# A hybrid decoder layer on one core: the groups' stage written as a fixed order of slots on three engines

## The chip, the core and the metric

The kernel runs on one core of a Trainium2 chip. Four engines of that core matter here: TensorE (PE in the profile) multiplies matrices into PSUM, ScalarE (ACT) evaluates functions and copies, VectorE (DVE) does arithmetic on tiles, and SyncE (SP) issues the loads of the weights. GpSimd (POOL) issues a few other loads. Each engine has its own list of instructions and works through it in order; an instruction that needs another engine's result waits on a semaphore, and everything behind it on that engine waits too. The metric is the time of one execution of the program on the device, in microseconds (us).

## The reference: what is computed

The layer takes 512 tokens of width 1024 with 16 learned tokens in front (528 positions). After a norm, one projection gives five parts: a pooled branch, the gate `z`, the inputs `x`, `B`, `C` of a state-space branch (Mamba-2, in chunks of 128 tokens), the step `dt`, and two sets of sigmoid gates. The state-space branch has 32 heads of 64 channels in 8 groups of 4 heads:

```python
xbc = silu(causal_depthwise_conv(xbc, conv_w, conv_b))       # x, B, C; 4 taps
a_cs = cumsum(dt * a) per chunk
lmat = exp(a_cs[l] - a_cs[s]) for s <= l, else 0             # decay between two tokens
y_diag = (C B^T * lmat) @ (x * dt)                           # inside a chunk
states = B^T @ (exp(a_cs[-1] - a_cs) * x * dt)               # what a chunk hands on
y_off  = C @ state_before * exp(a_cs)
y = (y_diag + y_off + x * d_skip) * silu(z)
y = y * rsqrt(mean(y * y over the group's 256 channels) + eps) * norm_w
```

The result of the 8 groups goes through `w_ssd_out`, is merged with the pooled branch by the gates, goes through `w_o` onto the residual, and an MLP with squared ReLU and a last norm follow. All is float32; products are made of a high and a low part of each operand (three products instead of one), so every block of weights is split on the chip into `whi` (a cast on ScalarE) and `wlo` (a subtraction on VectorE).

## The kernel before

**Blocks of weights.** All weights come as blocks of 128 x 1024. `block()` hands out the next one; `depth[0]` says how many more are loaded and split ahead of it, which is 2 in the groups' stage. A block is a load (SP, into one of three `raw` buffers), the cast on line 75 and the subtraction on line 76; `whi` and `wlo` have four buffers each.

**The groups' stage.** It is a loop over the 8 groups, one round each. In a round, the scan of group g (`ssd`, lines 397 to 522) and the projections of group g+1 (`group_proj`, line 364) are woven together. The scan's parts are: transposes of x and B (lines 413 to 434, tiles `ptb`, `ptm`, `ptx`), the decays (`eb`, lines 445 to 456: the exponentials, and between them the differences of cumulated decays in place in `abc`), the products C B^T and the states (`pcb`, `pst`), the outputs (`po` from the states, `py` from the masked decays), their gathering into `yt` on VectorE (lines 495 to 499), the sum of squares by a product with ones (`png`), and the norm and the split of the result into `yh` and `yl`. The projections are four tiles `px` (B, C and two of x, 48 products each, of 264 or 258 columns), a tile `pz` of twice 24 products of 512 columns, and in some rounds a gate `pgp` of 24 such products. A `px` tile goes through `conv` (line 342): one activation on ScalarE, three multiply-adds on VectorE that read it from PSUM, and a SiLU on ScalarE.

**Rounds that differ.** Round 4 also multiplies the first 8 results with half of `w_ssd_out` (`out_half`, tiles `pso`, copied on ScalarE to `acc`), and round 7 has no projections and multiplies results 8 to 13 instead (`out_part`, tiles `psp`, added on VectorE to `acc`). `GATE_AT` says which rounds have a gate.

**What sets the order.** Both parts are generators, and `weave` runs them in turn by the counts of `STEPS`: that is the order on TensorE alone (`manual_schedule` names PE only). On ScalarE and VectorE the framework's scheduler picks the order by its own estimate of when operands are ready. PSUM holds two tiles of 1024 columns (`psum2`, for `px`, `pz`, `pgp`, `pso`, `psp`) and four of 512 (`psum1`, for the scan); a tile is written anew when what read the old one is done.

## Time and profile before

| | us |
|---|---|
| median of three runs | 1037.05 (1034.16 to 1037.66) |
| the profiled execution | 1034.4 |
| its span, first to last instruction | 1032.7 |
| groups' stage in it (first transposes of round 0 to the end of the last `psp` tile) | 66.9 to 485.4 |
| busy in the span: PE, DVE, ACT | 1007.3, 714.5, 562.7 |

A matrix product is shown as busy until its modelled end, which lies after the start of the next one, so a full row of PE says that products follow each other, not that they are at their peak. PEclk is the clock that was granted to TensorE; below 1.00 its products take longer. A row of the view of waits says who waited for whom, for how long in total, how often, and the longest wait.

### The profile page before, as it was taken

Reading aid. Unit: us, or ns where it says so; the run is one execution under the profiler, and the core shown is the slowest. Engines: PE = TensorE matmul, PEld = TensorE weight load, DVE = VectorE, ACT = ScalarE, POOL = GpSimd, SP = SyncE. Lnnn points to the kernel's source line nnn. Section 1 sums busy time; section 2 is a strip of 40 time slices with the busy share of each in tenths; the row PEclk is TensorE's granted clock in tenths of the full one; section 3 lists DMA queues with packets and bytes.
Section 4 is the critical chain, followed back from the end, with each engine's and each line's share of the span. In section 5 each row is a group of like instructions: output and inputs, shape, how many; then the busy total and the mean of one; then the engine's idle time right before and its main releaser. Section 6 shows DMA issues by size and latency. Waiting matters only on the chain.

```text
span 1032.7 us, 14079 instructions
## 1 busy us (share of the span) xinstructions
PE 1007.3 (98%) x5689; PEld 874.0 (85%) x5689; DVE 714.5 (69%) x950; ACT 562.7 (54%) x748; POOL 88.6 (9%) x52
## 2 busy tenths in 40 slices
PE   9999999999889999989999999999999999999997
PEld 8888889898678898968899888888888888888886
DVE  7988676776535585967756457875777567666866
ACT  7774959577526629582334333374554345454444
POOL 0100000000000000000000000002131422403400
PEclk9999999999899999999999999999999999999999
DMA  6243141423322231413532333324323323233112
GB/s 236 73 156 105 34 148 41 144 62 128 97 76 109 87 118 42 144 37 106 205 102 83 104 100 100 125 82 146 100 82 122 105 92 110 102 103 123 41 42 82
DMA packets 29281, 105.62 MB, mean 102 GB/s; under 512 B 3296, under 2 KB 4256, under 8 KB 28192
## 3 DMA queue, kind: packets, MB, share of 16 engines
q1 hardware_dynamic: 26496, 92.75, 27.7%
q0 software_dynamic: 2000, 11.08, 2.8%
q8 instruction: 44, 0.72, 0.3%
q10 hardware_dynamic: 720, 0.91, 0.3%
q14 instruction: 21, 0.17, 0.1%
HBM read 102.55 MB, written 2.16 MB: 101 GB/s over the span
## 4 chain that ended last, share of the span: by engine, by line
PE 82%; ACT 9%; DVE 6%; issue 2%; DMA 1%; SPq 0%; ACTq 0%; DVEq 0%
PE pf L96 6%; PE pf L98 6%; PE pf L97 6%; PE px L154 4%; PE px L155 4%; PE px L157 4%; PE alpha L985 3%; PE alpha L987 3%; PE alpha L986 3%; PE pz L154 2%; PE pz L157 2%; PE pz L155 2%; PE pp L157 1%; PE pp L154 1%; PE pp L155 1%
## 5 line engine op out<-in xcount | busy, mean ns | idle before, releaser
L76 DVE TENSOR_TENSOR wlo<-raw,whi 128x1024 fp32r<-128x1024 f32 (+1 forms) x131 | 163.3, 1252 | 146.8 <-ACT whi L75 146.8
L75 ACT CAST whi<-raw 128x1024 fp32r<-128x1024 f32 (+1 forms) x131 | 135.7, 1043 | 219.2 <-PE pf L97 55.8
L154 PE MATMUL px<-uh,whi 128*128 128x264 f32 (+1 forms) x448 | 120.2, 289 | 4.1 <-DVE bt L347 2.5
L155 PE MATMUL px<-ul,whi 128*128 128x264 f32 (+1 forms) x448 | 117.3, 283 | 0.0
L96 PE MATMUL pf<-vh,whi 128*128 128x512 f32 x256 | 99.8, 390 | 0.0
L98 PE MATMUL pf<-vh,wlo 128*128 128x512 f32 x256 | 99.6, 389 | 0.0
L97 PE MATMUL pf<-vl,whi 128*128 128x512 f32 x256 | 99.6, 389 | 0.0
L157 PE MATMUL px<-uh,wlo 128*128 128x264 f32 (+1 forms) x448 | 90.4, 283 | 0.0
L154 PEld LDWEIGHTS px<-uh,whi 128*128 128x128 f32 x448 | 84.7, 189 | 5.7 <-issue 3.7
L155 PEld LDWEIGHTS px<-ul,whi 128*128 128x128 f32 x448 | 84.4, 188 | 0.2
L747 DVE TENSOR_TENSOR slo<-b,shi 128x1024 fp32r<-128x1024 f32 x35 | 49.2, 1404 | 31.6 <-ACT shi L746 31.6
L157 PEld LDWEIGHTS px<-uh,wlo 128*128 128x128 f32 x448 | 68.8, 188 | 0.0
L746 ACT CAST shi<-b 128x1024 fp32r<-128x1024 f32 x35 | 36.8, 1050 | 47.3 <-PE pf L97 36.4
L98 PEld LDWEIGHTS pf<-vh,wlo 128*128 128x128 f32 x256 | 48.1, 188 | 10.0
L97 PEld LDWEIGHTS pf<-vl,whi 128*128 128x128 f32 x256 | 48.1, 188 | 10.0
L96 PEld LDWEIGHTS pf<-vh,whi 128*128 128x128 f32 x256 | 48.1, 188 | 9.8
L996 POOL TENSOR_TENSOR b<-b,b 128x1024 f32<-128x1024 f32 x14 | 35.5, 2539 | 238.3 <-DVE slo L747 238.3
L985 PE MATMUL alpha<-shi,hh 128*128 128x512 f32 x140 | 54.6, 390 | 0.0
L987 PE MATMUL alpha<-shi,hl 128*128 128x512 f32 x140 | 54.5, 389 | 0.0
L986 PE MATMUL alpha<-slo,hh 128*128 128x512 f32 x140 | 54.5, 389 | 0.0
L812 DVE TENSOR_TENSOR ht<-ht,alpha 128x1024 f32<-128x1024 f32 x35 | 42.6, 1217 | 10.9 <-PE alpha L987 10.9
L154 PE MATMUL pz<-uh,whi 128*128 128x512 f32 x112 | 44.0, 392 | 1.8 <-DVE xc L347 1.4
(419 smaller groups left out, 2497.8 us busy)
## 6 DMA issues: line engine op xcount, KB each, us to landing
raw<-in_w SPq DMA_DIRECT2D x129, 512.0 KB, 3.5
b<-in_w SPq DMA_DIRECT2D x28, 512.0 KB, 3.5
abc<-acs_d POOLq DMA_DIRECT2D x8, 1024.0 KB, 5.6
wob<-in_w SPq DMA_DIRECT2D x8, 512.0 KB, 5.2
xt<-in_xT SPq DMA_DIRECT2D x8, 264.0 KB, 5.9
ht<-in_x POOLq DMA_DIRECT2D x4, 512.0 KB, 6.2
w<-in_w SPq DMA_DIRECT2D x4, 512.0 KB, 3.5
out_dram<-out SPq DMA_DIRECT2D x4, 320.0 KB, 2.4
```

Source lines behind the costliest of these rows:

```text
L75: act.copy(hi[:, c], raw[:, c])
L76: dve.tensor_tensor(lo[:, c], raw[:, c], hi[:, c].bitcast(F32), op=ALU.subtract)
L96: pe.matmul(ps, ah, bh, start=first, stop=False)
L97: pe.matmul(ps, ah, bl, start=False, stop=False)
L98: pe.matmul(ps, al, bh, start=False, stop=last)
L154: pe.matmul(o, wh, rhs[0][k][:, c], start=k == 0, stop=False)
L155: pe.matmul(o, wh, rhs[1][k][:, c], start=False, stop=False)
L157: pe.matmul(o, wl, rhs[0][k][:, c], start=False, stop=k == NK - 1)
L747: dve.tensor_tensor(lo, src, hi.bitcast(F32), op=ALU.subtract)
L985: pe.matmul(ps[t], a[0], wh[:, cs], start=f, stop=False, skip_group_check=True)
L986: pe.matmul(ps[t], a[0], wl[:, cs], start=False, stop=False, skip_group_check=True)
L987: pe.matmul(ps[t], a[1], wh[:, cs], start=False, stop=l, skip_group_check=True)
```

## The change

The generators and `weave` go. The scan becomes a class `Scan` with a method for each part, and one loop calls these parts and the projections in a written order. `manual_schedule` now names PE, Activation and DVE, so that this order is kept on all three engines, the splits of the weights and the copies of `acc` included.

- The SiLU of B, C and x leaves `conv` and is done for the three tiles at the end of the round, x in one instruction (`silus`).
- All 16 decay differences of a round are Relu activations on ScalarE (`spans`); before, 8 were there and 8 on VectorE (line 453). The exponentials that follow, and the multiplication with the masked product C B^T on VectorE (`scores`), are done in two halves.
- Of the sum of squares, `squares` stands after the convolution of the fourth `px` tile, and the product with ones (`norm`) between the two halves of `pz`; before, it stood behind both.
- In rounds with a gate, root and result (`root`, `finish`) are done in the round, and the gate's product is now the last one of the round. In rounds 0 and 5, which have none, they are left to the next round (`late`), after its transposes and its first `px` tile.
- The gate of round 5 moves to round 6, and the blocks of weights are stored in the new order.
- In round 4, `out_half` is no longer mixed with the projections: the eight products come first, then the four `px` tiles.

**The start of the stage, on VectorE.** The last instructions ahead of the groups' stage and the first of it. `m_2` is the third gate of the stage before; `bm`, `xdm`, `xm`, `xdt`, `xdd` are made from the transposes of round 0; the first `px` tile multiplies with the first of the `wlo` that stand here. Before:

```order
L76 TENSOR_TENSOR wlo_885<-raw_883,whi_884 128x1024
L338 TENSOR_TENSOR ul_108<-xt_138,uh_100 128x528
L338 TENSOR_TENSOR ul_109<-xt_139,uh_101 128x528
L541 TENSOR_TENSOR m_1_123<-pgp_711,rsb 128x512
L338 TENSOR_TENSOR ul_110<-xt_140,uh_102 128x528
L76 TENSOR_TENSOR wlo_891<-raw_889,whi_890 128x1024
L76 TENSOR_TENSOR wlo_897<-raw_895,whi_896 128x1024
L541 TENSOR_TENSOR m_2_124<-pgp_744,rsb 128x512
L424 TENSOR_TENSOR xdm_829<-ptm_840,decm 16x256
L76 TENSOR_TENSOR wlo_982<-raw_980,whi_981 128x1024
```

And now:

```order
L548 TENSOR_TENSOR m_2_124<-pgp_744,rsb 128x512
L424 TENSOR_TENSOR bm<-ptb_831,bm 16x128
L428 TENSOR_TENSOR xdm_829<-ptm_840,decm 16x256
L430 CAST xm<-xdm_829 16x256
L431 CAST xm<-xdm_829 16x256
L432 TENSOR_TENSOR xm<-xdm_829,xm 16x256
L439 TENSOR_TENSOR xdt_828<-ptx_0_847,dtok 128x512
L439 TENSOR_TENSOR xdt_828<-ptx_1_853,dtok 128x512
L443 TENSOR_TENSOR xdd_859<-xdt_828,dec 128x768
L76 TENSOR_TENSOR wlo_864<-raw_862,whi_863 128x1024
L76 TENSOR_TENSOR wlo_870<-raw_868,whi_869 128x1024
L76 TENSOR_TENSOR wlo_876<-raw_874,whi_875 128x1024
```

Three subtractions stood ahead of `m_2`, among the instructions of the stage before, and a fourth behind `xdm`; now the first three stand behind the eight instructions that use the transposes. Their casts on ScalarE moved in the same way, behind those for `bm` and `btok`.

**The end of a round, on VectorE.** `xc` is the convolution of the fourth `px` tile (three instructions), `sqg` the sum of squares and `qlg` its low part, for which TensorE's product with ones waits. Before (round 0):

```order
L76 TENSOR_TENSOR wlo_1236<-raw_1234,whi_1235 128x1024
L347 SCALAR_TENSOR_TENSOR xc_822<-px_3_1132,vs,xc_822 128x527
L504 TENSOR_TENSOR sqg_1196<-sqg_1196 128x512
L347 SCALAR_TENSOR_TENSOR xc_822<-px_3_1132,vs,xc_822 128x526
L247 TENSOR_TENSOR qlg_1200<-sqg_1196,qhg_1199 128x512
L347 SCALAR_TENSOR_TENSOR xc_822<-px_3_1132,vs,xc_822 128x525
```

And now (round 1; all rounds but 4 and 7 end alike):

```order
L347 SCALAR_TENSOR_TENSOR xc_1270<-px_5_1573,vs,xc_1270 128x527
L347 SCALAR_TENSOR_TENSOR xc_1270<-px_5_1573,vs,xc_1270 128x526
L347 SCALAR_TENSOR_TENSOR xc_1270<-px_5_1573,vs,xc_1270 128x525
L76 TENSOR_TENSOR wlo_1643<-raw_1641,whi_1642 128x1024
L516 TENSOR_TENSOR sqg_1671<-sqg_1671 128x512
L247 TENSOR_TENSOR qlg_1675<-sqg_1671,qhg_1674 128x512
L76 TENSOR_TENSOR wlo_1683<-raw_1681,whi_1682 128x1024
```

The sum of squares stood between the three instructions of the convolution; now it stands behind all three and behind one split of weights.

**The beginning of round 1, on ScalarE.** `zt` is the SiLU that ends the round before, `rs` the root for group 0, `yh` the high part of its result, `eb` and `abc` the decays of group 1. Before:

```order
L391 ACTIVATE zt_825<-pz_1203 128x1024
L511 ACT_TABLE_LOAD
L511 ACTIVATE rs_1268<-png_1265,eps 128x512
L415 COPY btok_1289<-ptb_1290 128x384
L512 ACT_TABLE_LOAD
L512 ACTIVATE rs_1268<-rs_1268 128x512
L418 CAST bm<-ptb_1290 16x128
L419 CAST bm<-ptb_1290 16x128
L450 ACTIVATE abc_1285<-abc_1285,dtok 128x128 x2
L519 CAST yh_0_1272<-yt_1099 128x512
L450 ACTIVATE abc_1285<-abc_1285,dtok 128x128
L519 CAST yh_1_1277<-yt_1099 128x512
```

And now:

```order
L676 ACTIVATE zt_827<-pz_1193 128x1024
L421 CAST bm<-ptb_1277 16x128
L422 CAST bm<-ptb_1277 16x128
L423 COPY btok_1276<-ptb_1277 128x384
L75 CAST whi_1309<-raw_1308 128x1024
L526 ACT_TABLE_LOAD
L526 ACTIVATE rs_1362<-png_1234,eps 128x512
L527 ACT_TABLE_LOAD
L527 ACTIVATE rs_1362<-rs_1362 128x512
L535 CAST yh_0_1366<-yt_1097 128x512
L535 CAST yh_1_1371<-yt_1097 128x512
L450 ACTIVATE eb_1375<-abc_1268 64x1024 x2
```

The casts for `bm` and `btok`, on which VectorE's work on the transposes rests, now come ahead of the root; `eb`, which had been computed in the round before, comes behind it, and with it everything that follows for group 1.

The diff, cut to its core:

```diff
--- before.py
+++ after.py
@@ -39,7 +39,7 @@
 
 
 GATES_FIRST = 3
-GATE_AT = {1: 3, 2: 4, 3: 5, 5: 6}
+GATE_AT = {1: 3, 2: 4, 3: 5, 6: 6}
...
-        act.activation(dst, dst, AF.Silu)
+
+    def silu(t):
+        act.activation(t, t, AF.Silu)
...
+    def xbc_tile(g, cur, n):
+        dst, t, skip = tiles_of(g, cur)[n]
+        runs, view = wide(psum2(f"px{g}_{t}"), skip)
+        proj(runs, block(), U)
+        return lambda: conv(dst, view, t)
+    def z_half(ps, i):
+        proj(narrow(ps[:, i * SEQ : (i + 1) * SEQ]), block(), U)
...
+        def turn(self):
...
+            pbm = ptb[:NM, 3 * P :]
+            act.copy(bm[hi], pbm)
+            act.copy(bm[mid], pbm)
+            act.copy(self.btok.rearrange("p c n -> p (c n)"), ptb[:, : 3 * P])
+            dve.tensor_tensor(bm[low], pbm, bm[hi].bitcast(F32), op=ALU.subtract)
...
+        def spans(self, rs):
+            for r in rs:
+                for c in range(4):
+                    h = R * self.g + r
+                    act.activation(self.dm[:, r, c, :], self.dm[:, r, c, :], AF.Relu, scale=-1.0,
+                                   bias=dtok[:, 1, c, h : h + 1])
+
+        def decays(self, i):
+            d = self.abc[:, 2 * i : 2 * i + 2]
+            act.activation(d, d, AF.Exp, scale=-1.0)
...
+        def scores(self, i):
+            d = self.abc[:, 2 * i : 2 * i + 2, :]
+            dve.tensor_tensor(d, d, self.cbm.rearrange("p c l -> p (c l)").unsqueeze(1)
+                              .to_broadcast([P, 2, SEQ]), op=ALU.mult)
...
...
-                if r < 2:
-                    act.activation(dm[:, r, c, :], dm[:, r, c, :], AF.Relu, scale=-1.0,
-                                   bias=dtok[:, 1, c, R * g + r : R * g + r + 1])
-                else:
-                    dve.tensor_scalar(dm[:, r, c, :], dm[:, r, c, :], dtok[:, 1, c, R * g + r : R * g + r + 1],
-                                      0.0, op0=ALU.subtract, op1=ALU.min)
-        act.activation(abc[:, :2], abc[:, :2], AF.Exp, scale=-1.0)
-        act.activation(abc[:, 2:], abc[:, 2:], AF.Exp)
...
+        def squares(self):
+            sq = gs.tile([P, 2, SEQ], F32, tag="eb", name=f"sqg{self.g}")
+            act.activation(sq, self.yt, AF.Square)
+            dve.tensor_tensor(sq[:, 0, :], sq[:, 0, :], sq[:, 1, :], op=ALU.add)
+            self.q = col_sums(f"g{self.g}", sq[:, 0, :], gs, ("qh", "ql"))
+
+        def norm(self):
+            self.pn = psum1(f"png{self.g}")
+            for n in range(2):
+                pe.matmul(self.pn, ones_r, self.q[n], start=n == 0, stop=n == 1)
+
+        def root(self):
+            self.rs = gs.tile([P, SEQ], F32, tag="cbm", name=f"rs{self.g}")
+            act.activation(self.rs, self.pn, AF.Ln, bias=eps, scale=1.0 / 256)
+            act.activation(self.rs, self.rs, AF.Exp, scale=-0.5)
+
+        def finish(self):
...
-    def weave(a, b, counts):
-
-        end = object()
-        for _, n in zip(a, counts):
-            while n and b:
-                if next(b[0], end) is end:
-                    b.pop(0)
-                else:
-                    n -= 1
...
+    half = {}
+
+    def out_half(d):
+        if d % 2 == 0:
+            half[0] = psum2(f"pso{d}")
+        ps = half[0][:, (d % 2) * SEQ : (d % 2 + 1) * SEQ]
+        ssd_out(d, ps, range(8))
+        act.copy(acc[d], ps)
...
-    STEPS = {3: (1, 1, 1, 1, 1, 1, 0), 4: (2, 2, 2, 2, 2, 4, 0), 7: (2, 2, 0, 2, 1, 1, 0)}
+    half = {}
+
+    def out_half(d):
+        if d % 2 == 0:
+            half[0] = psum2(f"pso{d}")
+        ps = half[0][:, (d % 2) * SEQ : (d % 2 + 1) * SEQ]
+        ssd_out(d, ps, range(8))
+        act.copy(acc[d], ps)
+
+    part = units()
+
+    def out_part(d):
+        ps = psum2(f"psp{d}")[:, :SEQ]
+        for k in range(8, 14):
+            mm3(ps, next(part), ys[k], k == 8, k == 13)
+        dve.tensor_tensor(acc[d], acc[d], ps, op=ALU.add)
+
     depth[0] = 2
-    with tc.manual_schedule(engines={mybir.EngineType.PE}):
+    late = None
+    with tc.manual_schedule(engines={mybir.EngineType.PE, mybir.EngineType.Activation, mybir.EngineType.DVE}):
         for g in range(G):
-            nxt = group_tiles(g + 1) if g + 1 < G else None
-            fill = [group_proj(g + 1, nxt, GATE_AT.get(g))] if nxt else [out_part()]
-            if g == 4:
-                fill = [out_half()] + fill
-            weave(ssd(g, cur), fill, STEPS.get(g, (1, 1, 1, 1, 2, 0, 0)))
+            sc = Scan(g, cur)
+            last = g + 1 == G
+            if not last:
+                nxt = group_tiles(g + 1)
+                tile_ = lambda n: xbc_tile(g + 1, nxt, n)
+            sc.turn()
+            if last or g == 4:
+                step = out_part if last else out_half
+                sc.spread()
+                step(0)
+                sc.spans((0, 1))
+                sc.states()
+                step(1)
+                sc.decays(0)
+                sc.spans((2,))
+                step(2)
+                sc.spans((3,))
+                sc.decays(1)
+                sc.scores(0)
+                sc.scores(1)
+                sc.outputs()
+                step(3)
+                sc.gather(0)
+                step(4)
+                sc.gather(1)
+                sc.squares()
+                step(5)
+                step(6)
+                sc.norm()
+                step(7)
+                sc.root()
+                sc.finish()
+                if last:
+                    break
+                convs = tile_(0)
+                convs()
+                tile_(1)()
+                tile_(2)()
+                tile_(3)()
+            else:
+                after = tile_(0)
+                if late is not None:
+                    late.root()
+                    late.finish()
+                    late = None
+                sc.spread()
+                after()
+                sc.states()
+                after = tile_(1)
+                sc.spans((0, 1))
+                sc.decays(0)
+                sc.spans((2,))
+                after()
+                after = tile_(2)
+                sc.spans((3,))
+                sc.decays(1)
+                sc.scores(0)
+                sc.scores(1)
+                after()
+                sc.outputs()
+                after = tile_(3)
+                sc.gather(0)
+                sc.gather(1)
+                after()
+            gate = GATE_AT.get(g)
+            xc, bt, ct, zt = nxt
+            silus = lambda: [silu(t) for t in (bt, ct, xc.rearrange("p i t -> p (i t)"))]
+            ps = psum2(f"pz{g + 1}")
+            z_half(ps, 0)
+            if g != 4:
+                sc.squares()
+                if gate is None:
+                    silus()
+                    late = sc
+                sc.norm()
+            z_half(ps, 1)
+            if gate is not None:
+                sc.root()
+                sc.finish()
+            if g == 4 or gate is not None:
+                silus()
+            act.activation(zt.rearrange("p i t -> p (i t)"), ps, AF.Silu)
+            if gate is not None:
+                gate_pool(gate)
             cur = nxt
     depth[0] = 0
...
             put(cols(w_in, OFF_XBC + t * P))
+        for j in range(2):
+            put(cols(w_in, OFF_Z + (2 * g + j) * P))
         if gate_d is not None:
             gate(gate_d)
-        for j in range(2):
-            put(cols(w_in, OFF_Z + (2 * g + j) * P))
 
     def wg(b):
         put(w_g[2 * b : 2 * b + 2].reshape(2, 2, P, 256).transpose(2, 0, 1, 3).reshape(P, 1024))
```

## The prediction

> **What bounds the kernel now.** I read the page first, then TensorE's waits in the groups' stage, then windows, then single instructions in order of time.

> ```profile
> PE 1007.3 (98%) x5689; PEld 874.0 (85%) x5689; DVE 714.5 (69%) x950; ACT 562.7 (54%) x748; POOL 88.6 (9%) x52
> ```

> TensorE is the bound, and the change leaves every product of it in place. So only its stops can change. In the window of the stage they are:

> ```profile
> PE pso L96 <- ACT acc L574: 7.5, 4, 4.1
> PE psp L96 <- ACT yh L519: 3.2, 1, 3.2
> PE px L154 <- DVE bt L347: 2.5, 1, 2.5
> PE px L154 <- ACT ct L344: 1.6, 1, 1.6
> PE pz L154 <- DVE xc L347: 1.4, 1, 1.4
> ```

> That is 16.2 us in eight stops: 2.5 in round 1, 1.6 in round 0, 3.2 in round 7, the rest in round 4. The groups of the transposes' line add five short stops:

> ```profile
>   DVE xdm L424: 1.5, 5
> ```

> The windows show the whole stage, and the three stretches in which the clock was below 1.00 (the ninth number):

> ```profile
> 66.86:485.37 418.51, 401.44 (x2706) 361.57 (x2705) 284.73 (x449) 265.27 (x358) 3.70 (x7) 0.99 0.28 93
> 255.00:270.00 15.00, 10.92 (x55) 8.91 (x54) 9.70 (x18) 14.82 (x25) 0.00 (x0) 0.93 0.25 70
> 270.00:285.00 15.00, 15.00 (x62) 12.38 (x62) 8.48 (x11) 3.40 (x5) 0.00 (x0) 0.84 0.34 106
> 450.00:465.00 15.00, 11.73 (x49) 9.10 (x48) 9.79 (x14) 12.85 (x23) 0.00 (x0) 0.89 0.11 36
> ```

> The clock cost 15 x (0.07 + 0.16 + 0.11) = 5.1 us, after the stop of 4.1 and at that of 3.2. These rows give the pieces of a round:

> ```profile
> 60.05 0.39 PE L154 MATMUL pgp<-xh,whi 128*128 128x512 f32 x1
> 60.27 0.39 PE L155 MATMUL pgp<-xl,whi 128*128 128x512 f32 x1
> 68.30 0.37 PE L154 MATMUL px<-uh,whi 128*128 128x264 f32 x1
> 68.87 0.40 PE L157 MATMUL px<-uh,wlo 128*128 128x264 f32 x2
> 74.20 1.05 PE L461 MATMUL pcb<-ct,bt 128*128 128x128 f32 x8
> 76.32 0.47 PE L154 MATMUL px<-uh,whi 128*128 128x258 f32 x1
> 89.93 1.95 PE L485 MATMUL po<-ct,st 128*128 128x128 f32 x16
> 93.70 0.39 PE L154 MATMUL px<-uh,whi 128*128 128x264 f32 x1
> ```

> Products of 512 columns follow at some 0.226 us but are shown for 0.39: a real stop costs 0.16 more than its idle time. A half of `pz` is 24 x 0.226 = 5.4 us, a `px` tile 74.20 - 68.30 = 5.9, the transposes 68.30 - 66.86 = 1.4, the states 2.1, the outputs 3.8 (`po` and `py` half each). All stops together cost 16.2 + 8 x 0.16 + 1.5 + 5.1 = **24.1 us**: no reordering of this stage can gain more. I take them all out and put in the stops of the written order.

> **The change, part by part.** The durations on the other two engines, grouped over the stage (busy, then mean ns):

> ```profile
> L76 DVE TENSOR_TENSOR wlo<-raw,whi 128x1024 fp32r<-128x1024 f32 x58 | 70.3, 1221 | 71.5 <-ACT whi L75 71.5
> L476 DVE TENSOR_TENSOR abc<-abc,cbm 128x2048 f32<-128x2048 f32 x8 | 18.3, 2286 | 4.2 <-ACT abc L455 4.2
> L347 DVE SCALAR_TENSOR_TENSOR xc<-px,vs,xc 128x527 f32<-128x527 f32 x14 | 10.6, 760 | 0.0
> L474 DVE TENSOR_TENSOR st<-st,cdec 128x256 f32<-128x256 f32 x24 | 10.0, 418 | 0.4 <-ACT st L472 0.3
> L516 DVE SCALAR_TENSOR_TENSOR yt<-yt,vs,rs 128x512 f32<-128x512 f32 x14 | 9.9, 749 | 10.0 <-ACT rs L512 10.0
> L520 DVE TENSOR_TENSOR yl<-yt,yh 128x512 fp32r<-128x512 f32 x14 | 9.4, 688 | 1.6 <-ACT yh L519 1.5
> L439 DVE TENSOR_TENSOR xdd<-xdt,dec 128x768 f32<-128x768 f32 x8 | 7.7, 959 | 0.3
> L428 DVE TENSOR_TENSOR xm<-xdm,xm 16x256 fp32r<-16x256 f32 x8 | 3.3, 416 | 0.3
> L420 DVE TENSOR_TENSOR bm<-ptb,bm 16x128 fp32r<-16x128 f32 x8 | 2.3, 282 | 0.4
> L75 ACT CAST whi<-raw 128x1024 fp32r<-128x1024 f32 x58 | 59.9, 1045 | 88.3 <-PE px L155 32.2 <-PE pso L97 26.9 <-DMA raw<-in_w 8.8
> L450 ACT ACTIVATE abc<-abc,dtok 128x128 f32<-128x128 f32 x64 | 20.2, 390 | 0.2
> L445 ACT ACTIVATE eb<-abc 64x1024 f32<-64x1024 f32 x16 | 16.9, 1059 | 0.2
> L344 ACT ACTIVATE xc<-px,vs 128x528 f32<-128x528 f32 x14 | 11.0, 783 | 0.0
> L349 ACT ACTIVATE xc<-xc 128x528 f32<-128x528 f32 x14 | 9.0, 646 | 25.5 <-DVE xc L347 25.5
> L511 ACT ACT_TABLE_LOAD x7 | 9.0, 1283 | 0.1
> L519 ACT CAST yh<-yt 128x512 fp32r<-128x512 f32 x14 | 8.1, 608 | 0.0
> L391 ACT ACTIVATE zt<-pz 128x1024 f32<-128x1024 f32 x7 | 7.2, 1024 | 0.1
> L511 ACT ACTIVATE rs<-png,eps 128x512 f32<-128x512 f32 x7 | 4.8, 689 | 0.1
> 67.06 0.69 DVE L541 TENSOR_TENSOR m<-pgp,rsb 128x512 f32<-128x512 f32 x1 [1.74 <-PE pgp L157]
> ```

> What they show is the price of each step, and that neighbours overlap: 64 Relus take 20.2 us, 0.316 each, though one lasts 0.390. What has no row here I price by the row of its kind and size.

> *Costed at nothing.* Eight more Relus a round put 2.5 us on ScalarE and take eight small steps from VectorE, and 20 of 52 table loads go (counted in the order), 25.7 us of ScalarE. Both lie beside TensorE's products; without that cover, in rounds 1 and 6, they are inside the chains below. SP's loads keep their kind and count, only a gate's block goes behind two others; three `raw` buffers still lead by two blocks. GpSimd's load of `abc` still starts when `py` of the round before is done, 17 us ahead of its use.

> *The start of round 0.* The first `wlo` now stands behind the work on the transposes. From the end of `m_2` (67.75) VectorE needs 0.28 + 0.41 + 2 x 0.28 + 0.42 + 2 x 0.69 + 0.96 + 1.22 = 5.2 us, so the first low product runs at 73.0 instead of 68.87: **4.2 us**. TensorE stands still for 1.6 us until the first `whi`, does four products, and stands another 2.4. The clock fell where 3.2 us of the 3.4 before it were idle, and after the stop of 4.1; it did not at the stop of 2.5. Here some 4 us in 4.7 are idle, so I add one stretch like that of window 450, 15 x 0.11 = **1.7 us** (bounds: nothing, as at the stop of 2.5, and 3.4, as after the longest). [...]

> *The end of rounds 0, 2, 3 and 5.* TensorE reaches the second product with ones 5.4 + 0.2 us after the fourth `px` tile, 5.5 after that tile's last product is written. In that time come, in one chain: activation 0.78, three multiply-adds 2.28, one `wlo` 1.22, sum 0.69, cast 0.61, subtraction 0.69, and five hand-overs between engines of some 0.02 each, 6.4 in all. That stops TensorE for 0.85 us, four times: **3.4 us**. Before, the product with ones came 10.9 us after the tile or later. VectorE's two gatherings in front (5.7) just fit: they start when the third tile's convolution and a split are done, and end some 0.4 us before that activation does.

> *Rounds 1 and 6, behind a round without a gate.* ScalarE has from the end of `pz`: `zt` 1.0, casts for `bm` 0.5, `btok` 0.4, a `whi` 1.05, two table loads and two activations for the root 3.9, the result of group g-1 with VectorE in turn 0.75 + 0.6 + 0.7 + 0.75 + 0.6, `eb` 2.1, and only then the activation of the new B, done 13.2 us after the round began, when TensorE is in its second tile. From there VectorE has 2.3 + 0.7 + 6 x 0.42 + 1.2 + 2.3 + 1.2 + 2.3 us of convolution, masked product, states, splits, convolution and scores: 25.7. TensorE wants the second half of the scores at 1.4 + 5.9 + 2.1 + 2 x 5.9 + 0.75 x 3.8 = 24.1, stops 1.6, and at the round's end VectorE has 2.3 + 1.2 + 5.7 + 2.3 + 1.2 + 0.7 + 0.6 + 0.7 = 14.7 more before the product with ones, against TensorE's 0.95 + 5.9 + 5.4 + 0.2 = 12.5: 2.2 more. **3.8 us a round, 7.6.**

> *Round 4.* Its stops after the copies of `acc` go where the states or the outputs lie between two products (two of four); the others cost about 0.7 (cast 0.6 and hand-overs) and 0.3 (the product with ones covers the rest). The outputs wait for the copy, four Relus, an exponential and half the scores, 0.2 + 0.6 + 1.25 + 1.05 + 1.15 = 4.2 after the third product, when they need it after 2.8: 1.4. The third `px` tile needs the first one's convolution, behind `root` and `finish`: 0.8. With 0.1 at the second product: **3.3 us**, and no stop that turns down the clock.

> *Round 7.* With the gate moved to round 6, its first product has all operands when the transposes are done, so the 3.2 us and their clock go. But ScalarE comes 3.2 us late out of a round with a gate (root, result, SiLUs, sigmoid: 14.2 us from the product with ones, against 10.9 on TensorE), so `xdd` is ready at 7.6 where the states want it at 6.5, and the scores come 0.4 late: **1.4 us**. In rounds 2 to 4 the longer first tile covers the same delay.

> *Sum.* In: 4.2 + 1.7 + 3.4 + 7.6 + 3.3 + 1.4 = 21.6. Out: 24.1. The profiled execution took 1034.4, so the changed kernel takes 1034.4 - 2.5 = **1031.9 us**. That execution lies 2.65 us below the median of the three runs, 1037.05; a difference that more half-clock stretches would make, and the new order has fewer long stops to cause them. So I leave the number as it is.

> **The rivals.** *VectorE's list is later than counted* (slower). In a written order each step follows the one that it depends on, while the rows are means over a mixed order; the Relus show that a neighbour that need not wait saves 0.07 us. Some 35 dependent steps a round at that price are 2.5 us. After the 0.4 us of slack in front of the fourth tile's convolution, 2.1 us would fall on the product with ones in each of six rounds: 12.6 more, **1044.5**. It decides from (2.5 + 3.1) / 6 + 0.4 = 1.3 us a round on. Against it: conv, states and gathering were chains of dependent steps before, too, and VectorE is 69% busy.

> [...]

> *The waits at the product with ones are hidden*, because overlaps shorten the chains by the 0.07 us a step that are not counted: 3.4 and 2 x 2.2 us less, **1024.1**. For it speaks that most steps are priced at full duration; against it, that the chain has five hand-overs.

> **How the numbers follow.** Forecast 0.42, with its own range 1028 to 1036; clock up 0.12; hidden waits 0.18; VectorE late 0.28. A difference of 0.3%, 3.1 us, is about what measuring this kernel can tell from no change. Faster by more: half of the forecast's range against the profiled execution, and more against the median, 0.2, most of the second, 0.1, and all of the third, 0.18: 0.48. Slower by more: the last without its mild end, 0.25, and 0.02 of the forecast's: 0.27. The rest is 0.25. The range of 8 in 10 reaches from just under the hidden waits to nearly the late VectorE: 1022 to 1043.

> **What would show it.** Right: TensorE stops ahead of the first `px` tile of round 0 for some 4 us, at `png` in rounds 0 to 3, 5 and 6, longest in 1 and 6, and at `py` in rounds 1, 4 and 6; no stop over 3 us in rounds 4 and 7; ScalarE 19 or 20 tables fewer. Wrong: a stop at `px` for a convolution in most rounds (VectorE behind), a second stretch of half clock, or a wait for `raw` loads.

## The result and the profile after

The changed kernel took 1039.68 us (median of 8 runs, 1038.64 to 1040.6) against 1036.42 for the kernel before in as many: a ratio of 1.0036, 95% interval 1.0025 to 1.0048. It is slower: by 0.31% in the medians and by 0.36% in the means, from which the ratio is taken, so at the edge of the 0.3% that the prediction set as its bound. A gain, 1031.9, was forecast; 1039.68 lies outside the forecast's own range of 1028 to 1036 and inside the wider one of 1022 to 1043. The profiled execution took 1040.55, its span is 1037.6, and the groups' stage takes 432.88 us of it where it took 427.45. Here the stage ends when the last `psp` product is followed by the next stage's first, at 494.31 us before and 499.06 now; the 485.4 given ahead of the prediction as the end of the last `psp` tile lies 9 us too early. One execution of all those below, of the kernel with three repairs, took 5429 us, and that run's median is given without it (1021.78 with it).

TensorE's waits in the stage, kernel after (us in total, times, longest):

```profile
PE px L157 <- DVE wlo L76: 3.6, 1, 3.6
PE png L522 <- ACT qhg L246: 3.5, 6, 1.3
PE ptx L438 <- DVE bm L424: 2.5, 2, 1.2
PE px L154 <- ACT whi L75: 1.6, 1, 1.6
...
PE png L522 <- DVE qlg L247: 1.4, 6, 0.2
PE pst L477 <- DVE xdd L443: 1.3, 4, 0.6
...
PE py L502 <- ACT whi L75: 1.1, 2, 0.5
```

The long waits behind the copies of `acc` (7.5 us) and for `yh` (3.2) are gone. In their place stand many short ones, in nearly every round. The windows cut the stage into rounds 0 to 7; the number behind the window is a round's length, the third from the end the granted clock. Before:

```profile
66.86:111.00 44.14, 42.50 (x321) 39.79 (x320) 32.74 (x59) 29.24 (x40) 0.53 (x1) 1.00 0.30 99
111.00:162.08 51.08, 48.42 (x344) 44.17 (x343) 36.32 (x60) 38.50 (x56) 0.53 (x1) 1.00 0.29 94
162.08:210.44 48.36, 48.17 (x344) 44.12 (x343) 35.93 (x57) 35.49 (x48) 0.53 (x1) 1.00 0.30 99
210.44:258.43 47.99, 47.92 (x344) 44.20 (x343) 36.43 (x56) 35.11 (x43) 0.53 (x1) 1.00 0.28 93
258.43:357.10 98.67, 89.68 (x513) 77.28 (x511) 48.32 (x72) 51.05 (x74) 0.53 (x1) 0.97 0.29 94
357.10:405.20 48.10, 47.98 (x345) 44.13 (x344) 32.36 (x52) 26.33 (x37) 0.53 (x1) 1.00 0.27 88
405.20:447.73 42.53, 42.46 (x320) 39.69 (x319) 34.15 (x54) 29.61 (x37) 0.53 (x1) 1.00 0.31 100
447.73:494.31 46.58, 43.24 (x225) 35.52 (x223) 32.41 (x49) 25.01 (x36) 0.00 (x0) 0.96 0.25 80
```

After:

```profile
66.18:117.52 51.34, 45.76 (x321) 42.12 (x320) 34.98 (x48) 27.88 (x44) 0.54 (x1) 0.93 0.25 93
117.52:169.56 52.04, 48.73 (x344) 44.12 (x343) 37.26 (x53) 35.12 (x54) 0.53 (x1) 1.00 0.26 92
169.56:218.76 49.20, 48.52 (x345) 44.21 (x344) 36.01 (x50) 34.12 (x52) 0.53 (x1) 1.00 0.28 97
218.76:267.94 49.18, 48.52 (x344) 44.20 (x343) 36.01 (x50) 34.10 (x52) 0.53 (x1) 1.00 0.28 97
267.94:359.11 91.17, 87.17 (x513) 75.70 (x511) 45.77 (x58) 45.93 (x67) 0.53 (x1) 1.00 0.29 99
359.11:402.38 43.27, 42.84 (x321) 39.63 (x320) 32.02 (x45) 26.30 (x42) 0.53 (x1) 1.00 0.25 86
402.38:456.07 53.69, 50.40 (x345) 45.29 (x343) 37.27 (x53) 36.78 (x55) 0.53 (x1) 0.97 0.24 89
456.07:499.06 42.99, 41.78 (x224) 34.59 (x223) 29.89 (x42) 25.54 (x42) 0.00 (x0) 1.00 0.26 85
```

Rounds 4 and 7 gained 7.5 and 3.6 us. Round 0 lost 7.2, rounds 1 to 3 together 3.0, and rounds 5 and 6, between which the gate moved, 6.3 together. What a round takes when TensorE does not stop is seen in an experiment below (b2_copy_on_vector), where its busy time equals the length of every round but round 4:

```profile
66.34:108.61 42.27, 42.27 (x320) 39.71 (x319) 33.50 (x58) 31.95 (x42) 0.53 (x1) 1.00 0.29 103
108.61:156.32 47.71, 47.71 (x345) 44.21 (x343) 36.64 (x60) 39.49 (x53) 0.53 (x1) 1.00 0.31 100
...
251.74:339.41 87.67, 86.38 (x513) 75.61 (x512) 53.26 (x80) 45.98 (x64) 0.53 (x1) 1.00 0.33 103
...
429.39:470.33 40.94, 40.94 (x225) 34.62 (x223) 30.61 (x49) 23.68 (x33) 0.00 (x0) 1.00 0.29 90
```

42.27 without a gate, 47.71 with one, 40.94 for round 7. In round 4 stops are left there too, so its length without stops is an estimate: 42.27 and the 192 products of `out_half`, which follow each other at 0.2267 us, make 85.8. Against these lengths the excess is, in us:

| round | 0 | 1 | 2 | 3 | 4 | 5 | 6 | 7 | sum |
|---|---|---|---|---|---|---|---|---|---|
| before | 1.87 | 3.37 | 0.65 | 0.28 | 12.9 | 0.39 | 0.26 | 5.64 | 25.3 |
| after | 9.07 | 4.33 | 1.49 | 1.47 | 5.4 | 1.00 | 5.98 | 2.05 | 30.8 |
| forecast of after | 6.75 | 3.8 | 0.85 | 0.85 | 3.3 | 0.85 | 3.8 | 1.4 | 21.6 |

VectorE's instructions in order of time at the start of round 0 show what the forecast left out (start, duration, idle time before and its releaser):

```profile
66.38 0.69 DVE L548 TENSOR_TENSOR m<-pgp,rsb 128x512 f32<-128x512 f32 x1 [4.75 <-PE pgp L157]
68.47 0.28 DVE L424 TENSOR_TENSOR bm<-ptb,bm 16x128 fp32r<-16x128 f32 x1 [1.40 <-ACT btok L423]
...
71.63 0.96 DVE L443 TENSOR_TENSOR xdd<-xdt,dec 128x768 f32<-128x768 f32 x1
72.50 3.49 DVE L76 TENSOR_TENSOR wlo<-raw,whi 128x1024 fp32r<-128x1024 f32 x3
```

`bm` heads VectorE's work on the transposes, and it waited 1.40 us for ScalarE's copy of `btok`, which in ScalarE's list stands behind a sigmoid:

```profile
66.82 0.26 ACT L421 CAST bm<-ptb 16x128 fp32r<-16x128 f32 x1 [4.43 <-PE ptb L418]
67.08 0.26 ACT L422 CAST bm<-ptb 16x128 fp32r<-16x128 f32 x1
67.35 0.72 ACT L549 ACTIVATE m<-m,vs 128x512 f32<-128x512 f32 x1
67.98 0.46 ACT L423 COPY btok<-ptb 128x384 f32<-128x384 f32 x1
```

The cast that `bm` subtracts was done at 67.08, but `bm` began at 68.47, 0.03 us after the copy's end at 68.44. Both steps read the PSUM tile `ptb`; in the program they share nothing else. That the common tile made `bm` wait is the author's reading; no run gives the two steps separate tiles. Over all rounds of the changed kernel this wait came to 21.7 us:

```profile
L424 DVE TENSOR_TENSOR bm<-ptb,bm 16x128 fp32r<-16x128 f32 x8 | 2.3, 282 | 21.7 <-ACT btok L423 21.7
```

### The profile page after: what moved, and what is told of

Its sections match the earlier page's. It is cut to its first block, busy times and chain, and to the rows that moved or that the text cites. A ratio compares the mean times of both kernels' runs of the same rounds, so it can differ in the third digit from the quotient of the medians.

```text
span 1037.6 us, 14031 instructions
## 1 busy us (share of the span) xinstructions
PE 1010.7 (97%) x5689; PEld 875.6 (84%) x5689; DVE 712.6 (69%) x894; ACT 555.4 (54%) x785; POOL 88.7 (9%) x52
## 4 chain that ended last, share of the span: by engine, by line
PE 77%; DVE 13%; ACT 9%; issue 2%; DVEq 0%; ACTq 0%
PE pf L96 6%; PE pf L98 6%; PE pf L97 6%; PE px L154 4%; PE px L157 3%; PE px L155 3%; PE alpha L1068 3%; PE alpha L1070 3%; PE alpha L1069 3%; DVE wlo L76 2%; PE pp L157 1%; PE pp L154 1%; PE pp L155 1%; PE pgs L155 1%; PE pgs L154 1%
## 5 line engine op out<-in xcount | busy, mean ns | idle before, releaser
L76 DVE TENSOR_TENSOR wlo<-raw,whi 128x1024 fp32r<-128x1024 f32 (+1 forms) x131 | 163.5, 1251 | 112.8 <-ACT whi L75 108.2
L75 ACT CAST whi<-raw 128x1024 fp32r<-128x1024 f32 (+1 forms) x131 | 135.7, 1041 | 122.3 <-PE pf L97 55.8
L154 PE MATMUL px<-uh,whi 128*128 128x264 f32 (+1 forms) x448 | 121.4, 291 | 2.7 <-ACT whi L75 1.6
L155 PE MATMUL px<-ul,whi 128*128 128x264 f32 (+1 forms) x448 | 118.6, 286 | 0.0
L96 PE MATMUL pf<-vh,whi 128*128 128x512 f32 x256 | 99.8, 390 | 0.0
L97 PE MATMUL pf<-vl,whi 128*128 128x512 f32 x256 | 99.6, 389 | 0.0
L157 PE MATMUL px<-uh,wlo 128*128 128x264 f32 (+1 forms) x448 | 91.5, 286 | 3.6 <-DVE wlo L76 3.6
L154 PEld LDWEIGHTS px<-uh,whi 128*128 128x128 f32 x448 | 85.9, 192 | 4.4 <-ACT whi L75 1.8
L155 PEld LDWEIGHTS px<-ul,whi 128*128 128x128 f32 x448 | 85.5, 191 | 0.2
L157 PEld LDWEIGHTS px<-uh,wlo 128*128 128x128 f32 x448 | 69.7, 190 | 3.8 <-DVE wlo L76 3.8
L97 PEld LDWEIGHTS pf<-vl,whi 128*128 128x128 f32 x256 | 48.1, 188 | 10.0
L96 PEld LDWEIGHTS pf<-vh,whi 128*128 128x128 f32 x256 | 48.1, 188 | 9.8
L895 DVE TENSOR_TENSOR ht<-ht,alpha 128x1024 f32<-128x1024 f32 x35 | 42.5, 1215 | 10.9 <-PE alpha L1070 10.9
L344 ACT ACTIVATE xc<-px,vs 128x528 f32<-128x528 f32 x14 | 11.1, 790 | 65.6 <-PE px L157 65.6
```

Of the source, the lines that this page charges most:

```text
L75: act.copy(hi[:, c], raw[:, c])
L76: dve.tensor_tensor(lo[:, c], raw[:, c], hi[:, c].bitcast(F32), op=ALU.subtract)
L96: pe.matmul(ps, ah, bh, start=first, stop=False)
L97: pe.matmul(ps, ah, bl, start=False, stop=False)
L154: pe.matmul(o, wh, rhs[0][k][:, c], start=k == 0, stop=False)
L155: pe.matmul(o, wh, rhs[1][k][:, c], start=False, stop=False)
```

## The experiments

All times are medians; the ratio is to the kernel before, timed on the same chip in the same rounds (1035.83 to 1036.23 there), with its 95% interval. "After" is 1039.68. The runs come from four chips besides that of "after"; on all of them the kernel before lay within 0.6 us, so differences of less than that between runs say nothing.

### What holds the loss: places, or the order itself

**The first blocks ahead of the order.**

```diff
     depth[0] = 2
+    while len(ahead) <= depth[0]:
+        ahead.append(block_tiles())
+        block_part(ahead[-1], slice(0, 1024))
     late = None
```

> Theory of places: the loss sits in a few places, each with its own cause, and goes when the cause goes. Here the first three blocks of the stage are split ahead of the written order. In the changed kernel the stretch from the first transposes of round 0 to the end of its first px tile is 8.1 us longer than its products need (two stops of 1.56 and 3.58 us, the rest at a lower clock): all of it goes, 1039.7 - 8.1 = 1031.6 (1030 to 1033). Theory of the order: to keep ScalarE and VectorE to a written list costs in each round, and a repair at one place only moves the wait to the next; at least half of the 8.1 us comes back within round 0, 1036 or more.

1032.53, 0.9969 (0.9956 to 0.9982), as the theory of places had it. In the trace round 0 took 43.26 us instead of 51.34: all 8.1 us went, and nothing came back later in the round.

**The written order on TensorE alone.**

```diff
-    with tc.manual_schedule(engines={mybir.EngineType.PE, mybir.EngineType.Activation, mybir.EngineType.DVE}):
+    with tc.manual_schedule(engines={mybir.EngineType.PE}):
```

> The written order holds on TensorE alone, ScalarE and VectorE are ordered by the scheduler as before. Theory of places: the 8.1 us at the start go, and what TensorE's own order causes stays (the product with ones between the two halves of pz, about 1 us in each of seven rounds, and the transposes of rounds 1 and 6, 1.45 us each, which wait for a PSUM tile): 1028 to 1032. Theory of the order: nearly the whole excess goes, 31.8 us of it less the few in rounds 4 and 7: under 1024. Third possibility, that the scheduler finds a worse order for this program than the written one: over 1036.

1014.26, 0.9788 (0.9772 to 0.9805): 25.4 us less than after, by an edit of one line. The program, its instructions on TensorE and their order are the same; only the order on ScalarE and VectorE is the scheduler's. TensorE's waits in the stage that are left:

```profile
PE pso L96 <- ACT acc L581: 3.9, 2, 3.0
PE py L502 <- DVE abc L486: 0.7, 1, 0.7
```

My theory of places had said that the product with ones between the halves of `pz` would keep its stop, since TensorE's own order makes it. It did not. The end of round 6 on VectorE, after:

```profile
437.67 2.36 DVE L347 SCALAR_TENSOR_TENSOR xc<-px,vs,xc 128x527 f32<-128x527 f32 x3
439.94 1.22 DVE L76 TENSOR_TENSOR wlo<-raw,whi 128x1024 fp32r<-128x1024 f32 x1
441.07 0.68 DVE L516 TENSOR_TENSOR sqg<-sqg 128x512 f32<-128x512 f32 x1
442.44 0.69 DVE L247 TENSOR_TENSOR qlg<-sqg,qhg 128x512 fp32r<-128x512 f32 x1 [0.68 <-ACT qhg L246]
```

And with the scheduler's order:

```profile
418.94 0.76 DVE L347 SCALAR_TENSOR_TENSOR xc<-px,vs,xc 128x527 f32<-128x527 f32 x1
419.62 0.68 DVE L516 TENSOR_TENSOR sqg<-sqg 128x512 f32<-128x512 f32 x1
420.21 0.76 DVE L347 SCALAR_TENSOR_TENSOR xc<-px,vs,xc 128x526 f32<-128x526 f32 x1
420.99 0.69 DVE L247 TENSOR_TENSOR qlg<-sqg,qhg 128x512 fp32r<-128x512 f32 x1
421.60 0.76 DVE L347 SCALAR_TENSOR_TENSOR xc<-px,vs,xc 128x525 f32<-128x525 f32 x1
```

The sum of squares stands between the steps of the convolution, and one of these fills the time in which `qlg` has to wait for ScalarE.

**The sum of squares ahead of the fourth convolution.**

```diff
                 sc.gather(1)
+                sc.squares()
                 after()
...
             if g != 4:
-                sc.squares()
                 if gate is None:
```

> The sum of squares stands ahead of the convolution of the fourth px tile instead of behind it. Theory of places: the first half of pz with the product with ones takes 1.0 us more than its products need in rounds 0, 2, 3 and 5, 2.1 in round 1 and 3.7 in round 6 (half clock among it); these 9.8 us go, and the later convolution costs nothing, since its px tile is wanted again only after pz: 1039.7 - 9.8 = 1029.9 (1029 to 1033). Theory of the order: the chain at the round's end only changes its last link, and the convolution, 2 us later, is waited for instead: 1037 or more.

1036.21, 1.0000 (0.9991 to 1.0010): 3.5 of the 9.8 us. The waits at `png` vanish, and others grow, in rounds 2 and 7 (the wait for `xdd` was 1.3 in all, that for the SiLU of x new):

```profile
PE pst L477 <- DVE xdd L443: 3.4, 4, 1.9
...
PE ptm L427 <- ACT xc L351: 1.5, 2, 0.8
```

In round 7, which took 47.82 us instead of 42.99, a stretch of half clock came on top (the granted clock of the profiled execution was 0.994 over its span). Neither theory foresaw this mixture: the places are real, but a round that ends earlier meets a ScalarE that is not ready.

**The SiLU of z behind the next transposes' copies.**

```diff
-            sc.turn()
+            sc.turn(held)
...
             act.copy(self.btok.rearrange("p c n -> p (c n)"), ptb[:, : 3 * P])
+            if held is not None:
+                held()
```

> In rounds 0 and 5, which leave the root to the next round, the SiLU of z stands behind the casts for bm and the copy of btok of the next round instead of ahead of them. Theory of places: the transposes of rounds 1 and 6 wait 1.45 us each for the PSUM tile of ptb, which is free when bm is made; they would wait 0.4 to 0.8, and the rest of the round is as before: 1037.5 to 1038.7. Theory of the order: ScalarE's list of the round is as long as before, so the wait comes back at py or png: 1039 to 1040.

1040.48, 1.0044 (1.0029 to 1.0059): no gain. The wait at `ptx` fell from 2.5 to 1.5, and that at `py` for a split on ScalarE rose from 1.1 to 2.2, as the theory of the order had it.

### Which list

**TensorE and ScalarE in the written order** (VectorE left out of the set of engines).

> The written order holds on TensorE and ScalarE; VectorE is ordered by the scheduler. With TensorE alone 1014.3 was measured, with all three engines 1039.7. Theory that VectorE's list is what costs (the convolution of the fourth tile, a split and the sum of squares in one row; bm first, behind which xdm, xdt and xdd wait for ScalarE): most of the 25.4 us go, and what ScalarE's list does at the start (its casts of the first blocks behind those for the transposes), in rounds 1 and 6 and in round 4 stays, 1024 (1018 to 1028). Theory that ScalarE's list costs: 1033 to 1040.

1024.26, 0.9887 (0.9872 to 0.9901), where the first theory had 1024. So VectorE's list was worth 15.4 us and ScalarE's another 10.0, taken off in this order.

**TensorE and VectorE in the written order** (ScalarE left out).

> The written order holds on TensorE and VectorE; ScalarE is ordered by the scheduler. Theory that VectorE's list costs: the stop ahead of the first px tile of round 0 stays (its subtractions stand behind the work on the transposes), and the chain at the end of each round stays; only the stops at ptx and py in rounds 1 and 6 and part of round 4's go: 1032 to 1037. Theory that ScalarE's list costs: 1016 to 1022.

1054.59, 1.0179 (1.0163 to 1.0194): slower than with all three, which neither theory allowed. The scheduler puts ScalarE's work for the transposes later still, and VectorE's list stands behind `bm`:

```profile
L424 DVE TENSOR_TENSOR bm<-ptb,bm 16x128 fp32r<-16x128 f32 x8 | 2.3, 282 | 48.3 <-ACT btok L423 48.3
```

Taken off in this other order, ScalarE's list is worth minus 14.9 us and VectorE's 40.3. Neither list has a price of its own; it depends on the other.

**The same, with bm behind xm.**

```diff
-            dve.tensor_tensor(bm[low], pbm, bm[hi].bitcast(F32), op=ALU.subtract)
...
             dve.tensor_tensor(xm[mid], xdm, xm[hi].bitcast(F32), op=ALU.subtract)
+            dve.tensor_tensor(bm[low], pbm, bm[hi].bitcast(F32), op=ALU.subtract)
```

> The written order on TensorE and VectorE, ScalarE ordered by the scheduler (1054.6, in which bm waits for ScalarE 48.3 us in 8 instances), and bm behind xm. Theory that this run was slower than the one with all three lists because the scheduler puts ScalarE's casts for the transposes behind other work, and VectorE's list holds everything behind bm: the waits for xdd and half of those at px, po and py in rounds 1 and 6 go, some 10 us: 1044.5 (1042 to 1048). Theory that bm's wait only stands for a ScalarE that is late anyway: 1052 or more.

1044.74, 1.0085 (1.0070 to 1.0101): the move of one small instruction by four places gives 9.9 us here, and TensorE's waits for `xdd` (7.3 us) are gone. It is still 5.1 us slower than with all three lists; the wait at `png` for ScalarE's cast is 8.9 us in this run and in the one before it, 3.5 in after. What else makes up the 5.1 was not taken apart.

### Lists written better

**The first blocks ahead, and bm behind xm.** The two edits shown.

> The written order on all three engines with the first three blocks ahead of it (1032.5) and, in addition, bm behind xm instead of at the head of VectorE's work on the transposes. In the changed kernel bm waits for ScalarE 21.7 us in 8 instances. Theory that this wait matters only where TensorE waits for xdd at the states: 0.5 us in rounds 2 and 3, 0.8 in 4, 0.5 in 7 go, 1030.1 (1029 to 1031.5). Theory that VectorE's whole list of a round stands late because of it: 1026 or less.

1029.62, 0.9944 (0.9925 to 0.9963): 2.9 us from `bm`, in all three lists. The number is that of the first theory, but only in part for its reason. Against the trace with the first repair alone, rounds 2 to 4 are 1.3 us shorter together, which is the theory; round 6 is 1.85 us shorter, and there a stretch of half clock is missing (the granted clock over the span was 0.999, and 0.997 with the first repair alone) though the stop at `png` is the same (1.3 us).

**The first blocks ahead, and the sum of squares inside the convolution.**

```diff
-    def conv(dst, src, ct):
+    def conv(dst, src, ct, steps={}):
...
             dve.scalar_tensor_tensor(dst[:, o:], src[:, e + o - j : e + n - j],
                                      col(V_CW, ct * 4 + 3 - j), dst[:, o:], op0=ALU.mult, op1=ALU.add)
+            if j in steps:
+                steps[j]()
...
-                after()
+                after({1: sc.squares})
```

> The written order on all three engines with the first three blocks ahead of it (1032.5) and, in addition, the sum of squares between the multiply-adds of the fourth tile's convolution; bm stays at the head. Theory that the two repairs are independent: with both 1021.8 was measured, so 1032.5 - 10.7 + 2.4 = 1024 (1023 to 1026). Theory that they hang together, since a round that ends earlier finds bm's wait for ScalarE in its place: waits for xdd come in rounds 2 and 7 as when the sum of squares was moved ahead of the convolution, and it gains only the 3.5 us that were measured there: 1029 (1027 to 1031).

1025.58, 0.9901 (0.9886 to 0.9916): 6.95 us beyond the start's repair, nearer to independent repairs.

**All three.**

> The written order on all three engines, with its lists mended where the traces show a wait: the first three blocks ahead of it, bm behind xm instead of ahead of xdm, the sum of squares between the multiply-adds of the fourth tile's convolution instead of behind it. Theory that the order costs by what it puts behind a waiting instruction, and that a better list recovers it: 8.1 at the start, some 9.8 at the product with ones and 2.4 at the states go, some 3 come back as waits for ScalarE in rounds 2 and 7, as when the sum of squares was moved ahead of the convolution: 1023 (1020 to 1026). Theory that a written list costs whatever stands in it: over 1030.

1021.05, 0.9862 (0.9840 to 0.9883): 11.5 us beyond the start's repair, where the two alone add to 9.9. A written order need not lose, but this one, with three mended places, is still 6.8 us behind the scheduler's.

**The kernel before, with its program's order on all three engines.**

```diff
-    with tc.manual_schedule(engines={mybir.EngineType.PE}):
+    with tc.manual_schedule(engines={mybir.EngineType.PE, mybir.EngineType.Activation, mybir.EngineType.DVE}):
```

> The kernel before, with its order of the program kept on ScalarE and VectorE too, nothing else changed. Theory that keeping the two engines to the order in which the program is written is what costs, here 25.4 us: the kernel before gets slower as well, by 10 us or more, since each SiLU then holds ScalarE until the convolution on VectorE is done: 1046 or more. Theory that the loss is peculiar to the new list: 1031 to 1041.

1085.62, 1.0482 (1.0456 to 1.0508). The price is not peculiar to the new list; the old program, whose SiLUs follow their convolutions, pays twice as much (49.4 us). ScalarE's longest waits there are those of its SiLUs:

```profile
ACT xc L349 <- DVE xc L347: 43.3, 13, 4.0
ACT ct L349 <- DVE ct L347: 42.3, 7, 6.9
```

How much of the 49.4 us they make is not shown: TensorE's own longest waits there are 9.7 us for the first `whi` of the stage and 8.9 behind the copies of `acc`.

### The other two parts of the change

Both on the kernel that keeps TensorE's order alone (1014.26).

**Half of the differences back on VectorE.**

```diff
-                    act.activation(self.dm[:, r, c, :], self.dm[:, r, c, :], AF.Relu, scale=-1.0,
-                                   bias=dtok[:, 1, c, h : h + 1])
+                    if r < 2:
+                        act.activation(self.dm[:, r, c, :], self.dm[:, r, c, :], AF.Relu, scale=-1.0,
+                                       bias=dtok[:, 1, c, h : h + 1])
+                    else:
+                        dve.tensor_scalar(self.dm[:, r, c, :], self.dm[:, r, c, :], dtok[:, 1, c, h : h + 1],
+                                          0.0, op0=ALU.subtract, op1=ALU.min)
```

> The written order on TensorE alone, as in the run that took 1014.3, and half of the decay differences back on VectorE, as before the change. Theory that the gain of that run is TensorE's new order, and the other parts of the change only move work that TensorE's products cover: 1014.3 within 3 us. Theory that the gain rests on VectorE being relieved of eight small steps a round: stops at py or png come back, 1019 or more.

1011.97, 0.9768 (0.9754 to 0.9783): 2.3 us less than with all of them on ScalarE, inside the 3 us that the first theory left open, but a gain.

**Each SiLU behind its convolution.**

```diff
-        return lambda: conv(dst, view, t)
+        def after():
+            conv(dst, view, t)
+            silu(dst)
+        return after
...
-            silus = lambda: [silu(t) for t in (bt, ct, xc.rearrange("p i t -> p (i t)"))]
+            silus = lambda: None
```

> The written order on TensorE alone, as in the run that took 1014.3, and each SiLU of B, C and x directly behind its convolution in the program, as before the change. Theory that the gain is TensorE's order: table loads come back on ScalarE (up to 20 at 1.28 us), covered by TensorE's products: 1014.3 within 3 us. Theory that the gain rests on ScalarE being relieved of them: the chain from pz to the next scores gets longer by two table loads and TensorE stops in most rounds, 1020 or more.

1012.10, 0.9768 (0.9752 to 0.9785). The stage has 63 table loads in this trace, 55 with the SiLUs at the round's end, 53 in the kernel before and 33 in the one after; the time goes the other way, and no run here shows a gain from fewer of them. In this trace TensorE waits 2.5 us in the whole stage, behind the copies of `acc`, so its products cover the loads.

**Both undone.**

> The written order on TensorE alone, and both other parts of the change undone: half of the differences on VectorE, each SiLU behind its convolution. Each undone alone took 1012.0 and 1012.1 against 1014.3. Theory that both gained in the same place, the stops behind the copies of acc in round 4 (6.2 us there with both parts, 3.1 with either undone): no more than either alone, 1011 to 1013. Theory that each takes its own work off a path: they add, 1009 to 1010.

1012.11, 0.9771 (0.9751 to 0.9791). They do not add: with either, the wait behind the copies of `acc` in round 4 falls from 3.9 to 2.5 us, and with both it is 2.5.

**And the copies of acc on VectorE.**

```diff
-        act.copy(acc[d], ps)
+        dve.tensor_copy(acc[d], ps)
```

> As the run before it, and the eight copies of acc in round 4 on VectorE instead of ScalarE. Theory that what is left of round 4's stops (3.1 us in the two runs that took 1012) comes from copies that stand behind other work in ScalarE's list: they go, about 3 us less than the run before, 1008 to 1010. Theory that VectorE's list holds the copies as long: no change, 1011 to 1013.

1010.65, 0.9757 (0.9740 to 0.9773), the fastest kernel here, 29 us under after. The gain of 1.5 lies between the two theories; of TensorE's waits in the stage 0.9 us behind a copy of `acc` and 0.4 us for a `whi` are left, both in round 4.

## Why the prediction was wrong, point by point

**What the stops before were worth** was nearly right: 24.1 us forecast, 25.3 by the rounds' lengths. They could be had, too: with TensorE's order alone the kernel takes 21.6 us less than before, most of it.

**Costed at nothing** was nearly right: with TensorE's order alone, undoing either part, which puts the table loads back or takes the Relus off ScalarE, gains 2.2 or 2.3 us, in rounds 4 and 7; the other rounds keep their length to 0.2 us. With all three lists it was not tried.

**What the written order puts in** is the step that failed: 30.8 us against 21.6. The sum took `bm`, the head of VectorE's list in each round, to wait for nothing, and the clock to fall for one stretch only.

- *The start of round 0.* 5.9 forecast for the stops and the clock (its 4.2 is 4.1 by its own figures); the experiment that takes the cause away gives 8.1. The sum began VectorE's list at the end of `m_2` and knew no wait of `bm` for ScalarE: 1.40 us, and the stop for `wlo` was 3.6 us instead of 2.4. What is left of the 8.1 after the two stops, 2.9 us, is the lower clock and the overlap that a stop loses; 1.7 was forecast, for one stretch of half clock, and two came, at 0.50 from 72.30 to 79.12.
- *The end of rounds 0, 2, 3 and 5* was right: 0.85 forecast, 1.00 in round 5, where nothing else stands.
- *Rounds 1 and 6.* 3.8 each forecast, 4.33 and 5.98 measured. The 2.2 us at `png` came (13.46 us from the end of the last `px` tile to the last product of `pz` in round 1, 2.1 above the 11.4 of a round without stops), those at `py` were 0.8 instead of 1.6, and 1.45 a round at `ptx` were not foreseen: a round whose root is left for later keeps a fourth PSUM tile, `png`, so that the transposes have to wait for `ptb`, and with it for `bm` (2.5 us of idle time in the two rounds). Round 6 paid a lower clock on top (0.97 over the round, 1.00 in round 1), the 1.65 us between the two.
- *Rounds 2 and 3.* 0.5 us each at the states, again `bm`, behind which `xdd` stands: not in the sum.
- *Round 4.* 3.3 forecast, 5.4 by the estimate above. The idle time is 0.9 us behind the copies (1.1 forecast), 1.4 at `py` (1.4) and 1.1 at `px` (0.8); 0.6 for `xdd` at the states was not in the sum, nor what a stop costs beyond its idle time.
- *Round 7.* 1.4 forecast, 2.05 measured. Of the wait for `xdd` in the sum 0.3 us came, and 0.8 behind an addition to `acc` (L589) was not in it.

So two things were left out. One is a small instruction at the head of VectorE's list that waits for another engine; it was read as a price of 0.28 us. The other is a second and a third stretch of half clock; the prediction itself names a second one as a sign of being wrong. The sum missed the stage by 7.9 us (5.4 longer, where 2.5 shorter was forecast). `bm` has 1.2 of them in the stop at the start, and moving it gave 1.3 in rounds 2 to 4 (the run with the first blocks ahead and `bm` behind `xm`); the lower clock has some 1.2 more than forecast in round 0, and 1.65 in round 6. The 1.85 us that the same run gained in round 6 are mostly that last stretch and are not counted again. How the remaining 2.5 us divide, the further stops of rounds 1, 4, 6 and 7 among them, was not taken apart.

**The rivals.** VectorE late had the sign right and the mechanism wrong: it put 2.1 us on the product with ones in each of six rounds beside the forecast's stops; 1.0 was found in four and 2.1 in two, as the forecast itself had it. Hidden waits: no, not in this order. The clock stays up at the start (the sum without its 1.7 us for the clock, 1030.2): no. It fell at 72.30, 2.1 us after the last of the four products and within the second stop, and was half for 6.8 us (kernel after; the number behind the length is the time for which TensorE was busy):

```profile
68.88:72.30 3.42, 0.76 (x4) 0.54 (x4) 3.26 (x7) 3.40 (x4) 0.00 (x0) 1.00 0.00 0
72.30:75.71 3.41, 1.94 (x9) 1.94 (x10) 3.41 (x4) 2.39 (x3) 0.00 (x0) 0.50 0.23 83
75.71:79.12 3.41, 3.41 (x17) 3.41 (x17) 0.28 (x1) 0.00 (x0) 0.00 (x0) 0.50 0.89 317
```

The four products within the stop, busy for 0.76 us of the first of these windows, did not keep it up.

What no term or rival asked was what another order on ScalarE and VectorE would do with the same program. The forecast priced the written order against the old trace and never against the scheduler's order of the new program; that comparison is the 25.4 us.

## What to carry to other kernels

Fix the order on the engine that bounds the kernel, and leave the engines that serve it to a scheduler unless their written lists have been looked at instruction by instruction: here the same edit gave 2% with one engine in the list and lost 0.4% with three. Where a list is fixed, look first at what stands at its head in each stage and for whom that waits, across engines, a shared PSUM tile included; here the place of one step of 0.3 us was worth 2.9 us in one order and 9.9 in another. Put between two dependent steps, whose hand-over goes through another engine, a step that waits for nothing.

## What the runs showed of the hardware

The half clock does not follow from the length of a stop alone. In rounds 1 and 6 of the changed kernel TensorE stopped alike at `png` (1.32 and 1.31 us of idle time, then 0.2); the clock stayed at 1.00 in the one and was halved in the other, while the kernel before kept it through a stop of 2.5 us.

In the groups' stage of the changed kernel the clock changed at 72.30, 79.12, 444.35 and 447.76, moments that lie 2, 107 and 1 times 3.4133 us apart; before, it changed at 267.97, 274.80, 455.70 and 459.12, which lie 2, 53 and 1 times that apart, all to 0.003 us. Windows of this length, laid out from these changes, show for how long TensorE was busy around each stop. Kernel after, in the window with round 1's stop, in that with round 6's, and in the one behind it:

```profile
154.22:157.63 3.41, 2.09 (x11) 1.40 (x9) 2.69 (x5) 0.71 (x2) 0.00 (x0) 1.00 0.06 22
440.94:444.35 3.41, 1.88 (x7) 1.18 (x7) 2.47 (x4) 2.54 (x3) 0.00 (x0) 1.00 0.48 154
444.35:447.76 3.41, 3.41 (x10) 2.66 (x9) 0.69 (x2) 2.91 (x4) 0.00 (x0) 0.50 0.47 161
```

And before, the stop of 2.5 us:

```profile
124.61:128.02 3.41, 2.21 (x19) 2.00 (x17) 3.41 (x5) 2.95 (x5) 0.00 (x0) 1.00 0.21 29
128.02:131.44 3.42, 2.14 (x18) 2.17 (x19) 3.42 (x7) 2.20 (x3) 0.00 (x0) 1.00 0.33 129
```

```profile
264.56:267.97 3.41, 1.01 (x5) 0.51 (x3) 1.83 (x3) 3.38 (x5) 0.00 (x0) 1.00 0.00 0
343.06:346.47 3.41, 1.97 (x16) 1.74 (x15) 3.41 (x5) 2.34 (x4) 0.00 (x0) 1.00 0.31 109
452.29:455.70 3.41, 0.20 (x1) 0.00 (x0) 1.71 (x4) 3.36 (x8) 0.00 (x0) 1.00 0.00 0
```

These three are of the kernel before; the clock fell behind the first and the third. That the place of a stop against the windows decides is the author's reading of two executions, which do not show where a line would lie; no run moved a stop alone. The stop of round 6 that halved the clock here did not when the first blocks stood ahead and `bm` behind `xm`: the granted clock over that run's span was 0.999, where it was 0.994 here, and its longest stop at `png` was 1.3 us as well.
